# Final norm: rows read ahead of the last two experts' sums, both experts' rows gathered and scattered apart

## The chip, the core and the metric

The kernel runs on one core of one Trainium2 chip, as one launch. The metric is device time in microseconds (us). The engines are TensorE (PE), VectorE (DVE), ScalarE (ACT), GpSimd (POOL) and SyncE (SP); SP does no arithmetic and issues most of the plain transfers, in its program's order. Indirect transfers (gather, scatter, scatter with add) are issued by POOL. Sixteen DMA engines move the data.

## The reference

One decoder block on 1024 tokens of width 1024, float32: attention, then a mixture of experts, then a last norm. What matters here is its end (cut):

```python
def _rmsnorm(x, g):
    y = x * lax.rsqrt(jnp.mean(x * x, axis=-1, keepdims=True) + NORM_EPS)
    return y * g
...
    h2 = _modulate(_rmsnorm(x, g_ffn[layer]), shift_ffn, scale_ffn).reshape(b * s, d)
    y = _hierarchical_moe(h2, ...)          # top group of 4, top 2 of its 8 experts
    x = x + gate_ffn[:, None, :] * y
    return _rmsnorm(x, g_final)
```

Each token gets the weighted outputs of two of the 32 experts (SwiGLU, inner width 512), added to its row; the row is then divided by its root mean square and multiplied by `g_final`.

## The kernel before

The program first computes attention and the routing, and leaves the rows of x, without the experts' part, in a DRAM tensor `acc` (1024 x 1024). The expert stage then runs over 32 places e = 0 to 31 (a table made on the chip says which expert stands at which place; every second place from 5 on has lists of up to 64 rows, the others up to 96; below, the expert at place e is called expert e). For each place POOL gathers the rows (`load_x`, L1220), PE turns them round (`xpose`), multiplies with 8 blocks of gate and up weights (`gate_up`) and 4 blocks of down weights (`down`); DVE multiplies by the gate row into `ys` (`finish`, L1322 and L1328), and POOL adds `ys` to the rows of `acc` by an indirect transfer (`add_rows`, L1337). A list `order` sets how the steps of neighbouring places mix. Weight blocks of 512 KB are loaded by SP (`load_to`, L974), up to 34 blocks ahead of their use; each of the last twelve waits for the load three before it.

Buffers of 128 x 1024 floats come from one pool of 49, taken in turn (`slot`). A framework adds the waits: for a buffer's last users, and between any two transfers that touch the same DRAM tensor when one of them writes it.

The tail, around the change: `finish(30)` issues the add of place 30 and then calls `f_load`, which lets SP read all of `acc` into eight buffers `fx0` to `fx7` (L1351), and lets POOL gather the rows of place 31 from `acc` into `xlast` (L1353). The sums of place 31 itself are never added in `acc`: `xl_add` (L1406) adds them to `xlast` on DVE. Then `f_square` (L1359, ACT) squares a tile and sums each row into a column of `ssf`; `rsqrt` (L172 to L187) makes the reciprocal roots of some columns, in 12 steps on DVE or 15 on POOL; `f_out` (L1364) multiplies on DVE, and SP writes 128 rows of the output (L1365). The rows of `xlast` are done the same way (column 8) and scattered over the output by POOL (L1369), behind all eight plain outputs, which wrote those rows without the sums of place 31.

The string `TAIL` sets the order of this part: sN is a square, rA-B roots of columns A to B-1 on DVE, gA-B the same on POOL, oN an output, y is `finish(31)`, x is `xl_add`. The squares of fx0 to fx2 stand ahead of it, between the down products of place 31. A last test (L1431 to L1438) asks whether any list ran over; the branch is not taken here.

Of the kernel before, what the change touches and what calls it, by code (L numbers as in the profile page):

```python
# [7 lines left out]
F32 = mybir.dt.float32  # L8
# [5 lines left out]
ALU = mybir.AluOpType  # L14
# [4 lines left out]
T = 1024  # L19
D = 1024  # L20
KT = 8
NE = 32
CAP = 96
CAPS = 64
# [33 lines left out]
UF = [1, 1, 1, 1, 1, 1, 0.98, 0.91]  # L58
GE = 'GGGG'
QS = "AS"  # L60
TAIL = "s3 s4 s5 r0-3 o0 y o1 g3-6 o2 s6 s7 x o3 o4 g6-9 o5 o6 o7 o8"
XA, TA, DA = 6, 4, 5
LLX = 34
LT = 0
# [32 lines left out]
def build(nc, tc, I, out, cap=CAP):  # L97
# [6 lines left out]
    cp = pool("const", 1)  # L104
# [5 lines left out]
    V, A, G, PE = nc.vector, nc.scalar, nc.gpsimd, nc.tensor  # L110
# [19 lines left out]
    def slot(name, dt=F32):  # L130
        return up.tile([128, D], dt, name=name, tag="u")
# [92 lines left out]
    for o in LOADS0.split():  # L224
        if o[0] == "w":
            i = int(o[1])
# [93 lines left out]
    acc = dp.tile([T, D], F32, name="acc")  # L320
# [285 lines left out]
    bc = {}  # L606
# [339 lines left out]
    EW, XE, ST, EREG = {}, {}, {}, {}  # L946
    capof = lambda e: CAPS if e in SMALL else cap
    listof = lambda e: (ls if e < NF else lsP)[:capof(e), e:e + 1]
# [119 lines left out]
    for k in range(KT):  # L1068
# [39 lines left out]
        for i in (0, 1):  # L1108
            hi, lo = wsp[i]
            for half in (0, 1):  # L1110
                c = slice(half * 512, half * 512 + 512)
# [11 lines left out]
    i = 0  # L1123
# [31 lines left out]
    for which in (0, 1):  # L1155
        qk_alloc(0, which)
        for half in (0, 1):
            c = slice(half * 512, half * 512 + 512)
# [7 lines left out]
    pend, last, fresh, late = list(range(NS)), [], set(), []  # L1166
    for s_ in range(NS + L7 + 1):
        if s_ < NS:
            p, i = divmod(s_, 16)
# [42 lines left out]
        last = todo  # L1212
# [101 lines left out]
    def finish(e):  # L1314
        st, c = ST.pop(e), capof(e)
        ps = st["y"]
        ys = slot(f"ys{e}")
        g = bc["gate2"]
        halves = [(slice(h * 512, h * 512 + 512), h) for h in (0, 1)]
        for n, h in halves:  # L1320
            r = slice(h * 64, h * 64 + 64)
            V.tensor_mul(ys[0:64, n], ps[r, 0:512], g[r, n])  # L1322
        if c > 64:
            t = slot(f"yt{e}")[0:64, 0:512]
            others(t, ps)
            for n, h in halves:
                r = slice(h * 32, h * 32 + 32)
                V.tensor_mul(ys[64:96, n], t[r], g[r, n])  # L1328
        if e == NE - 1:
            ST["last"] = ys  # L1330
        else:
            add_rows(e, ys)
        if e == NE - 2:
            f_load()

    def add_rows(e, ys):
        G.indirect_dma_start(out=acc[:], out_offset=bass.IndirectOffsetOnAxis(ap=listof(e), axis=0),  # L1337
# [1 line left out]
                             compute_op=ALU.add)  # L1339


    ssf = cp.tile([128, KT + 1], F32, name="ssf")
    rf = cp.tile([128, KT + 1], F32, name="rf")
    G.memset(ssf, 1.0)
    FX, FY = [], {}

    def f_load():
        load_to(len(wseq))
        for tt in range(KT):
            x = slot(f"fx{tt}")  # L1350
            nc.sync.dma_start(x, acc[tt * 128:tt * 128 + 128, :])  # L1351
            FX.append(x)
        G.indirect_dma_start(out=XL[:CAPS], out_offset=None, in_=acc[:],  # L1353
                             in_offset=bass.IndirectOffsetOnAxis(ap=listof(NE - 1), axis=0),
                             bounds_check=T - 1, oob_is_err=False)

    def f_square(tt, x, n=128):
        FY[tt] = slot(f"fy{tt}")
        A.activation(FY[tt][:n], x[:n], AF.Square, accum_out=ssf[:n, tt:tt + 1])  # L1359

    def f_out(tt):
        y = FY.pop(tt)
        if tt < KT:
            V.scalar_tensor_tensor(y, FX[tt], rf[:, tt:tt + 1], bc["final"], op0=ALU.mult, op1=ALU.mult)  # L1364
            nc.sync.dma_start(out[tt * 128:tt * 128 + 128, :], y)  # L1365
        else:
            V.scalar_tensor_tensor(y[:CAPS], XL[:CAPS], rf[:CAPS, tt:tt + 1], bc["final"][:CAPS],
                                   op0=ALU.mult, op1=ALU.mult)
            G.indirect_dma_start(out=out[:], out_offset=bass.IndirectOffsetOnAxis(ap=listof(NE - 1), axis=0),  # L1369
                                 in_=y[:CAPS], in_offset=None, bounds_check=T - 1, oob_is_err=False)  # L1370

    LL = LLX
    load_x(0)
# [6 lines left out]
    for o in order:  # L1380
        kind, e, i = o
        if kind in "GD":
            load_to(max(loaded[0], wpos[o] + LL - wpos[o] * LT // len(wseq)))
        if kind == "G":
            gate_up(e, i)
        elif kind == "X":
            xpose(e)
            if e + 1 < NE:
                scale_x(e + 1)
            if e + 2 < NE:  # L1390
                load_x(e + 2)
        elif kind == "T":
            act_t(e)
        elif kind == "D":
            down(e, i)
        elif kind == "Y" and e < NE - 1:
            finish(e)
        if o == ("G", NE - 2, 4):
            spread_row("final", cols[:, 72:80], G)
            XL = slot("xlast")  # L1400
            G.memset(XL[:CAPS], 0.0)
        if e == NE - 1 and kind == "D" and i:
            f_square(i - 1, FX[i - 1])

    def xl_add():
        V.tensor_add(XL[:CAPS], XL[:CAPS], ST["last"][:CAPS])  # L1406
        f_square(KT, XL, CAPS)

    sq_ = lambda tt: f_square(tt, FX[tt])
    rs_ = lambda a, b, eng=V: rsqrt(rf[:, a:b], ssf[:, a:b], b - a, 1.0 / D, eng)  # L1410
    for st in TAIL.split():
        k, a = st[0], [int(x) for x in st[1:].split("-") if x]
# [25 lines left out]
    with tc.If(rv > 0):  # L1438
# [15 lines left out]
        with tc.For_i(0, NE, 1) as e:  # L1454
# [6 lines left out]
            for tt in range(KT):  # L1461
                c = slice(tt * 128, tt * 128 + 128)
                x, xt, act, y, a = work2[tt % 2]
# [34 lines left out]
        for tt in range(KT):  # L1498
            x = fx[tt]
# [81 lines left out]
```

## Time and profile before

| | us |
|---|---|
| median of 3 runs | 1341.71 (1338.05 to 1342.66) |
| profiled execution | 1341.36 |
| its span | 1339.5 |
| busy in it: PE, DVE, ACT, POOL | 1170.3, 746.9, 520.3, 237.4 |
| data moved by DMA | 304.5 MB, mean 227 GB/s |

The span runs from the first to the last instruction; the execution's time is a little longer than it. A view of the profile names an instruction by engine, line and what it writes and reads (`fx<-acc`). "Landing" of a transfer is the time from its issue until its semaphore says that all is there. The chain that ended last is followed back from the last instruction, at each link to what released it, so it shows the work that sets the end; busy time of engines off that chain is not lost time.

### The profile page before, as it was taken

Reading aid. Unit: us, or ns where it says so; the run is one execution under the profiler, and the core shown is the slowest. Engines: PE = TensorE matmul, PEld = TensorE weight load, DVE = VectorE, ACT = ScalarE, POOL = GpSimd, SP = SyncE. Lnnn points to the kernel's source line nnn. Section 1 sums busy time; section 2 is a strip of 40 time slices with the busy share of each in tenths; the row PEclk is TensorE's granted clock in tenths of the full one; section 3 lists DMA queues with packets and bytes.
Section 4 is the critical chain, followed back from the end, with each engine's and each line's share of the span. In section 5 each row is a group of like instructions: output and inputs, shape, how many; then the busy total and the mean of one; then the engine's idle time right before and its main releaser. Section 6 shows DMA issues by size and latency. Waiting matters only on the chain. (4 is left out here: it accounts for less than half of the span.)

```text
span 1339.5 us, 19457 instructions
## 1 busy us (share of the span) xinstructions
PE 1170.3 (87%) x6848; PEld 688.1 (51%) x6848; DVE 746.9 (56%) x1484; ACT 520.3 (39%) x1023; POOL 237.4 (18%) x296
## 2 busy tenths in 40 slices
PE   4699989999999999799887999899999998888970
PEld 3497778778866886577665422223233222222320
DVE  6958773865497858878867233333333333332324
ACT  5246553655655445435422322233222222222212
POOL 3600000120100002313231110111111111111203
PEclk9799999999999999899998899999999999999985
DMA  9422442441001010456666799999999999999985
GB/s 353 161 77 95 149 154 95 142 85 42 32 17 48 16 64 0 149 214 236 229 250 228 253 334 359 336 386 377 367 372 373 376 375 374 376 377 388 359 276 200
DMA packets 89384, 304.54 MB, mean 227 GB/s; under 512 B 12417, under 2 KB 14849, under 8 KB 89282
## 3 DMA queue, kind: packets, MB, share of 16 engines
q1 hardware_dynamic: 81778, 282.00, 57.2%
q0 software_dynamic: 6352, 17.05, 5.4%
q10 hardware_dynamic: 1152, 4.19, 0.8%
q8 instruction: 56, 0.92, 0.3%
q14 instruction: 46, 0.38, 0.1%
HBM read 278.30 MB, written 29.63 MB: 230 GB/s over the span
## 5 line engine op out<-in xcount | busy, mean ns | idle before, releaser
L1264 PE MATMUL gu<-ew,xs 128*64 128x512 f32 x1024 | 252.1, 612 | 9.2 <-DMA ew<-we 5.2
L1322 DVE TENSOR_TENSOR ys<-y,bc_gate 64x512 f32<-64x512 f32 x64 | 44.0, 688 | 218.0 <-PE y L1271 129.0
L1264 PE MATMUL y<-ew,at 128*64 128x512 f32 x512 | 127.9, 629 | 12.1 <-DMA ew<-we 10.7
L1264 PEld LDWEIGHTS gu<-ew,xs 128*64 128x64 f32 x1024 | 63.6, 138 | 145.0 <-issue 73.1
L1241 ACT ACTIVATE xs<-xp,modc,affn 128x96 f32<-128x96 f32 (+1 forms) x128 | 52.0, 420 | 157.5 <-PE xp L1253 89.7
L549 PE MATMUL tp<-ident,P 128*128 128x128 f32 x576 | 89.1, 280 | 20.1 <-DVE P L533 9.6
L1337 POOL DMA_INDIRECT acc<-ys,lsP x27 | 38.7, 1434 | 377.7 <-DVE ys L1328 236.0
L532 DVE TENSOR_TENSOR_SCAN K<-K 128x1024 f32<-128x1024 f32 (+7 forms) x64 | 95.4, 1491 | 5.9 <-ACT K L520 5.7
L1264 PEld LDWEIGHTS y<-ew,at 128*64 128x64 f32 x512 | 35.8, 142 | 97.1 <-issue 45.3
L549 PEld LDWEIGHTS tp<-ident,P 128*128 128x128 f32 x576 | 65.7, 141 | 38.6 <-issue 9.4
L516 ACT ACTIVATE P<-P,st 128x1024 f32<-128x1024 f32 (+7 forms) x64 | 50.0, 781 | 91.3 <-DVE st L514 45.6
L573 PE MATMUL o<-PT,v 128*64 128x256 f32 (+1 forms) x640 | 74.9, 374 | 10.1 <-DVE PT L554 7.1
L1239 DVE TENSOR_SCALAR xs<-xp,affn,modc 128x96 f32<-128x96 f32 (+1 forms) x128 | 45.5, 363 | 57.8 <-ACT xs L1241 57.2
L210 DVE CUSTOM_DVE_ANT_0 wada<-wada,sc 128x1024 f32<-128x1024 f32 x48 | 64.4, 1354 | 9.7 <-DMA wada<-w_adaT 9.4
L520 ACT ACTIVATE K<-S 128x1024 f32<-128x1024 f32 (+7 forms) x64 | 41.9, 655 | 71.5 <-PE S L503 34.4
L1271 PE MATMUL gu<-ew,xs 128*32 128x512 f32 x576 | 69.3, 598 | 0.0
L514 DVE CUSTOM_DVE_ANT_0 P<-S,B 128x1024 f32<-128x1024 f32 (+7 forms) x64 | 48.3, 756 | 36.9 <-PE S L501 32.8
L1276 ACT ACTIVATE yt<-y 64x512 f32<-64x512 f32 x18 | 10.7, 595 | 143.4 <-PE xp L1253 127.1
L573 PEld LDWEIGHTS o<-PT,v 128*64 128x64 f32 x640 | 45.4, 141 | 40.1 <-DVE PT L554 9.7
L552 ACT ACTIVATE PT<-tp 128x512 f32<-128x512 f32 (+3 forms) x120 | 56.2, 496 | 15.4 <-PE tp L549 14.5
L533 DVE TENSOR_TENSOR P<-P,K 128x1023 f32<-128x1023 f32 (+7 forms) x64 | 51.6, 806 | 5.7 <-ACT P L521 0.7
L554 DVE COPY PT<-tp 128x512 f32<-128x512 f32 (+3 forms) x72 | 37.3, 537 | 16.1 <-PE tp L549 15.8
(637 smaller groups left out, 2510.0 us busy)
## 6 DMA issues: line engine op xcount, KB each, us to landing
ew<-we SPq DMA_DIRECT2D x384, 512.0 KB, 10.5
wada<-w_adaT SPq DMA_DIRECT2D x48, 512.0 KB, 6.0
wqk<-wqk SPq DMA_DIRECT2D x16, 512.0 KB, 3.6
xT<-xT SPq DMA_DIRECT2D x16, 256.0 KB, 5.5
wv<-wv SPq DMA_DIRECT2D x8, 512.0 KB, 7.7
B<-bias SPq DMA_DIRECT2D x8, 512.0 KB, 5.3
wo<-w_out SPq DMA_DIRECT2D x8, 512.0 KB, 4.9
x<-x SPq DMA_DIRECT2D x8, 512.0 KB, 4.7
```

The lines of the kernel that those rows point to most:

```text
L210: V.tensor_tensor_reduce(w, w, sc, op0=ALU.mult, op1=ALU.add, scale=1.0, scalar=0.0, accum_out=modc[:, v * 8 + k:v * 8 + k + 1])
L514: V.tensor_tensor_reduce(e, s, Bt[p, hd][:, :L], op0=ALU.add, op1=ALU.min, scale=-0.125, scalar=BIG, accum_out=st[:, 0:1])
L516: A.activation(e, e, AF.Exp, bias=st[:, 0:1], scale=-1.0, accum_out=st[:, 2:3])
L532: V.tensor_tensor_scan(k[:, :L], k[:, :L], k[:, :L], 1.0, op0=ALU.mult, op1=ALU.bypass)
L533: V.tensor_mul(b[:, 1:L], b[:, 1:L], k[:, 0:L - 1])
L549: PE.transpose(tp[:, jl - 4 * x, :], e[:, (jl - qo) * 128:(jl - qo) * 128 + 128], ident)
L552: A.activation(dst, tp[:, j0 - 4 * x:j1 - 4 * x, :], AF.Copy)
L573: PE.matmul(ps[hd * 64:hd * 64 + 64, 0:w], VV[p][:, j, hd * 64:hd * 64 + 64], pt[hd][jl // 4][:, jl % 4, 0:w], start=(n == 0), stop=(n == ...
L1239: V.tensor_scalar(dst, src, affn[:, k:k + 1], modc[:, 24 + k:25 + k], op0=ALU.mult, op1=ALU.add)
L1241: A.activation(dst, src, AF.Identity, scale=affn[:, k:k + 1], bias=modc[:, 24 + k:25 + k])
L1264: PE.matmul(ps[h * 64:h * 64 + 64, 0:512], a[:, i, 0:64], w[:, h * 512:h * 512 + 512], start=(i == 0), stop=(i == n - 1))
L1271: PE.matmul(ps[r:r + 32, 512:1024], a[:, j, 64:96], w[:, h * 512:h * 512 + 512], start=(j < 2), stop=(j >= n - 2))
```

## The change

`f_load` is called by `finish(29)`, ahead of the add of place 30, and no longer holds the gather. After the add of place 30, `finish(30)` issues two gathers from `acc`, the rows of place 30 and those of place 31 (`xlast30`, 96 rows, and `xlast31`, 64 rows). `fx0` to `fx7` hold the rows without the sums of places 30 and 31. Place 30's rows get column 8 of `ssf`, place 31's column 9, and both are scattered over the output, 30 first. `TAIL` changes: the square of `xlast31` comes ahead of s6, s7 and s8 (s8 is the square of `xlast30`), and the roots of columns 6 to 9 go from POOL to DVE.

```diff
--- before.py
+++ after.py
@@ -58,7 +58,7 @@
 UF = [1, 1, 1, 1, 1, 1, 0.98, 0.91]
 GE = 'GGGG'
 QS = "AS"
-TAIL = "s3 s4 s5 r0-3 o0 y o1 g3-6 o2 s6 s7 x o3 o4 g6-9 o5 o6 o7 o8"
+TAIL = "r0-3 o0 o1 s3 s4 s5 g3-6 o2 y x s6 s7 s8 o3 o4 o5 r6-10 o6 o7 o8 o9"
 XA, TA, DA = 6, 4, 5
 LLX = 34
 LT = 0
@@ -1330,8 +1330,13 @@
             ST["last"] = ys
         else:
             add_rows(e, ys)
-        if e == NE - 2:
+        if e == NE - 3:
             f_load()
+        elif e == NE - 2:
+            for i in (NE - 2, NE - 1):
+                G.indirect_dma_start(out=XL[i][:capof(i)], out_offset=None, in_=acc[:],
+                                     in_offset=bass.IndirectOffsetOnAxis(ap=listof(i), axis=0),
+                                     bounds_check=T - 1, oob_is_err=False)
 
     def add_rows(e, ys):
         G.indirect_dma_start(out=acc[:], out_offset=bass.IndirectOffsetOnAxis(ap=listof(e), axis=0),
@@ -1339,10 +1344,10 @@
                              compute_op=ALU.add)
 
 
-    ssf = cp.tile([128, KT + 1], F32, name="ssf")
-    rf = cp.tile([128, KT + 1], F32, name="rf")
+    ssf = cp.tile([128, KT + 2], F32, name="ssf")
+    rf = cp.tile([128, KT + 2], F32, name="rf")
     G.memset(ssf, 1.0)
-    FX, FY = [], {}
+    FX, FY, XL = [], {}, {}
 
     def f_load():
         load_to(len(wseq))
@@ -1350,9 +1355,6 @@
             x = slot(f"fx{tt}")
             nc.sync.dma_start(x, acc[tt * 128:tt * 128 + 128, :])
             FX.append(x)
-        G.indirect_dma_start(out=XL[:CAPS], out_offset=None, in_=acc[:],
-                             in_offset=bass.IndirectOffsetOnAxis(ap=listof(NE - 1), axis=0),
-                             bounds_check=T - 1, oob_is_err=False)
 
     def f_square(tt, x, n=128):
         FY[tt] = slot(f"fy{tt}")
@@ -1364,10 +1366,11 @@
             V.scalar_tensor_tensor(y, FX[tt], rf[:, tt:tt + 1], bc["final"], op0=ALU.mult, op1=ALU.mult)
             nc.sync.dma_start(out[tt * 128:tt * 128 + 128, :], y)
         else:
-            V.scalar_tensor_tensor(y[:CAPS], XL[:CAPS], rf[:CAPS, tt:tt + 1], bc["final"][:CAPS],
-                                   op0=ALU.mult, op1=ALU.mult)
-            G.indirect_dma_start(out=out[:], out_offset=bass.IndirectOffsetOnAxis(ap=listof(NE - 1), axis=0),
-                                 in_=y[:CAPS], in_offset=None, bounds_check=T - 1, oob_is_err=False)
+            e = NE - 2 + tt - KT
+            c = capof(e)
+            V.scalar_tensor_tensor(y[:c], XL[e][:c], rf[:c, tt:tt + 1], bc["final"][:c], op0=ALU.mult, op1=ALU.mult)
+            G.indirect_dma_start(out=out[:], out_offset=bass.IndirectOffsetOnAxis(ap=listof(e), axis=0),
+                                 in_=y[:c], in_offset=None, bounds_check=T - 1, oob_is_err=False)
 
     LL = LLX
     load_x(0)
@@ -1397,16 +1400,18 @@
             finish(e)
         if o == ("G", NE - 2, 4):
             spread_row("final", cols[:, 72:80], G)
-            XL = slot("xlast")
-            G.memset(XL[:CAPS], 0.0)
+            for i in (NE - 2, NE - 1):
+                XL[i] = slot(f"xlast{i}")
+                G.memset(XL[i][:capof(i)], 0.0)
         if e == NE - 1 and kind == "D" and i:
             f_square(i - 1, FX[i - 1])
 
     def xl_add():
-        V.tensor_add(XL[:CAPS], XL[:CAPS], ST["last"][:CAPS])
-        f_square(KT, XL, CAPS)
-
-    sq_ = lambda tt: f_square(tt, FX[tt])
+        x = XL[NE - 1][:CAPS]
+        V.tensor_add(x, x, ST["last"][:CAPS])
+        f_square(KT + 1, x, CAPS)
+
+    sq_ = lambda tt: f_square(tt, FX[tt]) if tt < KT else f_square(tt, XL[NE - 2], cap)
     rs_ = lambda a, b, eng=V: rsqrt(rf[:, a:b], ssf[:, a:b], b - a, 1.0 / D, eng)
     for st in TAIL.split():
         k, a = st[0], [int(x) for x in st[1:].split("-") if x]
```

What the built programs hold at three places follows. A row is line, operation, written from read, size, and the semaphores that it waits for: DMAHW0 to 7 are those of SP's transfers, taken in turn (fx0 to fx7 use 0 to 7, and so do the eight plain outputs), DMASW those of POOL's.

SP's queue, behind the weight loads, before: the last weight block and the reads of `acc`.

```order
L974 DMA ew31_11_10496<-we 128x1024 [waits DMAHW4_49,PE_49]
L1351 DMA fx0_10701<-acc_305 128x1024 [waits DMASW6_49,PE_49,Activation_49]
L1351 DMA fx1_10703<-acc_305 128x1024 [waits PE_49]
L1351 DMA fx2_10705<-acc_305 128x1024 [waits PE_49]
L1351 DMA fx3_10707<-acc_305 128x1024 [waits DVE_49]
L1351 DMA fx4_10709<-acc_305 128x1024 [waits DVE_49]
```

The same place in the changed program:

```order
L974 DMA ew31_11_10496<-we 128x1024 [waits DMAHW4_49,PE_49]
L1356 DMA fx0_10620<-acc_305 128x1024 [waits DMASW5_49,PE_49]
L1356 DMA fx1_10622<-acc_305 128x1024 [waits PE_49]
L1356 DMA fx2_10624<-acc_305 128x1024 [waits PE_49,Activation_49]
L1356 DMA fx3_10626<-acc_305 128x1024
L1356 DMA fx4_10628<-acc_305 128x1024 [waits PE_49]
```

The reads stand at the same place in SP's queue; the first waits for another add (DMASW5, place 29, instead of DMASW6, place 30).

POOL's queue from the clearing of `xlast` to the first roots, before:

```order
L1401 MEMSET xlast_10601 64x1024 [waits DMAHW3_49,DMAHW5_49,DMAHW2_49,PE_49]
L1337 DMA acc_305<-ys29_10612,lsP_316 1024x1024 [waits DMASW5_49,DMASW4_49,DVE_49]
L1337 DMA acc_305<-ys30_10690,lsP_316 1024x1024 [waits DMASW5_49,DVE_49]
L1353 DMA xlast_10601<-acc_305,lsP_316 64x1024 [waits DMASW7_49,DMASW6_49,Pool_49]
L172 TENSOR_SCALAR rs_10783<-ssf_7010 128x3 [waits Activation_49]
```

POOL's queue there in the changed program:

```order
L1405 MEMSET xlast30_10601 96x1024 [waits DMAHW3_49,DMAHW5_49,DMAHW2_49,PE_49]
L1405 MEMSET xlast31_10603 64x1024 [waits DMAHW4_49,PE_49]
L1342 DMA acc_305<-ys29_10614,lsP_316 1024x1024 [waits DMASW5_49,DMASW4_49,DVE_49]
L1342 DMA acc_305<-ys30_10708,lsP_316 1024x1024 [waits DMAHW3_49,DMAHW4_49,DMAHW2_49,DMAHW5_49,DMAHW1_49,DMAHW6_49,DMAHW0_49,DMAHW7_49,DMASW5_49,DVE_49]
L1337 DMA xlast30_10601<-acc_305,lsP_316 96x1024 [waits DMASW7_49,DMASW6_49,Pool_49]
L1337 DMA xlast31_10603<-acc_305,lsP_316 64x1024 [waits Pool_49]
L172 TENSOR_SCALAR rs_10785<-ssf_7010 128x3 [waits Activation_49]
```

The add of place 30 (`ys30`) now waits for all eight of SP's semaphores, at the values of the eight reads, and a second gather has come in behind it.

POOL's queue at the end of the changed program, from the last steps of its one set of roots on (before, a second set and one scatter stood there):

```order
L186 TENSOR_SCALAR rs_10785<-rs_10785 128x3 [waits Pool_49]
L187 TENSOR_TENSOR rf_7011<-rs_10785 128x3 [waits Pool_49]
L1372 DMA out<-fy8_10813,lsP_316 1024x1024 [waits DMAHW3_49,DMAHW4_49,DMAHW2_49,DMAHW5_49,DMAHW1_49,DMAHW6_49,DMAHW0_49,DMAHW7_49,DMASW1_49,DVE_49]
L1372 DMA out<-fy9_10807,lsP_316 1024x1024 [waits DMASW1_49,DVE_49]
L1442 TENSOR_LOAD cmi_10851 [waits DVE_49]
```

The first scatter waits for the eight plain outputs, as the one scatter did before; the second waits for the first (DMASW1).

ACT's squares, before:

```order
L1359 ACTIVATE fy3_10757,ssf_7010<-fx3_10707 128x1024 [waits DMAHW3_49]
L1359 ACTIVATE fy4_10759,ssf_7010<-fx4_10709 128x1024 [waits DMAHW4_49,Activation_49]
L1359 ACTIVATE fy5_10761,ssf_7010<-fx5_10711 128x1024 [waits DMAHW5_49,DMASW4_49,DMASW0_49]
L1359 ACTIVATE fy6_10801,ssf_7010<-fx6_10713 128x1024 [waits DMAHW6_49]
L1359 ACTIVATE fy7_10803,ssf_7010<-fx7_10715 128x1024 [waits DMAHW7_49]
L1359 ACTIVATE fy8_10806,ssf_7010<-xlast_10601 64x1024 [waits DMASW5_49,DMASW4_49,DVE_49]
```

ACT's squares in the changed program:

```order
L1361 ACTIVATE fy4_10781,ssf_7010<-fx4_10628 128x1024 [waits DMAHW4_49,DMASW4_49,DMASW0_49]
L1361 ACTIVATE fy5_10783,ssf_7010<-fx5_10630 128x1024 [waits DMAHW5_49]
L1361 ACTIVATE fy9_10807,ssf_7010<-xlast31_10603 64x1024 [waits DMAHW7_49,DVE_49]
L1361 ACTIVATE fy6_10809,ssf_7010<-fx6_10632 128x1024 [waits DMAHW6_49,DMASW5_49]
L1361 ACTIVATE fy7_10811,ssf_7010<-fx7_10634 128x1024 [waits DMAHW7_49]
L1361 ACTIVATE fy8_10813,ssf_7010<-xlast30_10601 96x1024 [waits DMASW7_49]
```

The square of the last place's rows, which waits for DVE's add, has moved ahead of those of fx6, fx7 and the second gathered tile.

## Rows read from the trace of the kernel before

**Rows 1.** The page: the span, and GB/s in 40 slices of it.
```profile
span 1339.5 us, 19457 instructions
...
GB/s 353 161 77 95 149 154 95 142 85 42 32 17 48 16 64 0 149 214 236 229 250 228 253 334 359 336 386 377 367 372 373 376 375 374 376 377 388 359 276 200
```

**Rows 2.** The chain that ended last: start us, length us, what.
```profile
1291.75 6.45 DMA acc<-ys,lsP
...
1300.08 8.75 DMA fx<-acc
...
1324.98 0.21 POOL rf L187
...
1327.72 2.63 DMA out<-fy
```

**Rows 3.** SP's own waits, 1230 to 1340: us in total, times, longest.
```profile
SPq L1351 <- DMA acc<-ys,lsP: 7.3, 1, 7.3
```

**Rows 4.** Timeline of ACT, 1255 to 1262: start us, length us, instruction.
```profile
1259.63 0.59 ACT L1289 ACTIVATE sg<-gu 64x512 f32<-64x512 f32 x1
```

**Rows 5.** Timeline of POOL, 1250 to 1340: the add of place 29.
```profile
1270.41 1.47 POOL L1337 DMA_INDIRECT acc<-ys,lsP x1 [6.34 <-DVE ys L1322]
```

**Rows 6.** Line 974 in 1290 to 1292, the last weight load: ns, start us; landing.
```profile
L974 SPq DMA_DIRECT2D ew<-we x1: 333/333/333, 1290.6 to 1290.6; - x1
...
DMA to landing us min/median/max: 4.1/4.1/4.1
```

**Rows 7.** Line 1351, the eight reads: ns min/median/max, first and last start; landing.
```profile
L1351 SPq DMA_DIRECT2D fx<-acc x8: 331/430/462, 1298.3 to 1301.6; - x8
...
DMA to landing us min/median/max: 4.2/8.8/10.9
```

**Rows 8.** A stretch: us, PE, PEld, DVE, ACT, POOL busy, clock, DMA share, GB/s.
```profile
1255.00:1260.00 5.00, 4.82 (x26) 1.25 (x26) 2.89 (x7) 2.60 (x5) 3.23 (x5) 1.00 1.02 417
```

**Rows 9.** Line 1353, the gather of place 31.
```profile
L1353 POOL DMA_INDIRECT xlast<-acc,lsP x1: 1012/1012/1012, 1299.0 to 1299.0; - x1
...
DMA to landing us min/median/max: 7.4/7.4/7.4
```

**Rows 10.** Line 1337, all 31 adds.
```profile
DMA to landing us min/median/max: 5.6/7.9/9.2
```

**Rows 11.** Line 1369, the scatter of place 31.
```profile
L1369 POOL DMA_INDIRECT out<-fy,lsP x1: 1011/1011/1011, 1331.2 to 1331.2; - x1
...
DMA to landing us min/median/max: 3.6/3.6/3.6
```

**Rows 12.** Line 1220, the 32 gathers of the expert stage.
```profile
DMA to landing us min/median/max: 4.6/8.1/10.5
```

**Rows 13.** Timeline of DVE, 1306 to 1330: roots, last sums, last two plain outputs.
```profile
1307.65 0.17 DVE L172 TENSOR_SCALAR rs<-ssf 128x3 f32<-128x3 f32 x1 [14.10 <-ACT fy L1359]
...
1309.64 0.16 DVE L184 SCALAR_TENSOR_TENSOR rf<-rs 128x3 f32<-128x3 f32 x1
...
1315.07 1.21 DVE L1406 TENSOR_TENSOR xlast<-xlast,ys 64x1024 f32<-64x1024 f32 x1
...
1325.22 2.48 DVE L1364 SCALAR_TENSOR_TENSOR fy<-fx,rf,bc_final 128x1024 f32<-128x1024 f32 x2 [3.44 <-POOL rf L187]
```

**Rows 14.** Timeline of ACT, 1300 to 1320: two squares in a row.
```profile
1310.14 1.06 ACT L1359 ACTIVATE fy<-fx 128x1024 f32<-128x1024 f32 x1
...
1311.29 1.06 ACT L1359 ACTIVATE fy<-fx 128x1024 f32<-128x1024 f32 x1
```

**Rows 15.** Timeline of POOL, 1310 to 1319: first, seventh and last step of one set of roots.
```profile
1311.39 0.19 POOL L172 TENSOR_SCALAR rs<-ssf 128x3 f32<-128x3 f32 x1 [11.40 <-ACT fy L1359]
...
1313.01 0.99 POOL L187 TENSOR_TENSOR rs<-rs 128x3 f32<-128x3 f32 x1
...
1317.87 0.19 POOL L187 TENSOR_TENSOR rf<-rs 128x3 f32<-128x3 f32 x1
```

**Rows 16.** Line 1575, the program's end: POOL's drains, ns min/median/max.
```profile
L1575 POOLq DRAIN  x3: 46/107/5381, 1333.3 to 1339.2; - x3
```

## The prediction

> **What bounds the kernel now.** I read the page first, then the chain that ended last, then the waits and the timeline of its stretch. The profiled execution took 1341.36 us around a span of 1339.5 us; the median of the three runs, 1341.71, is 0.35 us above it, so sums made on the profile may stand against the median as they are. Up to about 1295 us the expert stage streams weights at some 370 GB/s [rows 1], and nothing there is touched: the rows of PE stand in the same order in both programs, and every weight load stands where it stood. What the change reaches is the serial tail behind it. The reader is to see these links in it [rows 2]: the add of expert 30's rows takes 6.45 us from its start at 1291.75 to its landing at 1298.20; the eight reads of `acc` follow, with a link of 8.75 us; the reciprocal roots on POOL end at 1325.2; the last plain output leaves at 1327.72 and lands at 1330.35; then comes the scatter of the last expert's rows. The reads began late for one reason: SP waited 7.3 us for that add [rows 3]. This is the wait that the change takes away.
>
> **Part 1: the reads go earlier, by 7.4 us.** In the new program the first read waits for the add of expert 29, which starts at 1270.4 [rows 5], and for buffers whose last users are done at 1259.6, when expert 29's activation starts [rows 4]. But SP works in order, and ahead of the reads stand the weight loads, the last of which was issued at 1290.6 and took 0.33 us [rows 6]. So the reads start at 1290.9 where they started at 1298.3 [rows 7]. Before, the last of them was issued at 1301.6 and landed 10.9 us later, at 1312.5 [rows 7]; moved as a block by 7.4 us this is **1305.1**. Short end: the last weights land 4.1 us after 1290.6, at 1294.7 [rows 6], and eight reads then follow at the 1.23 us in which 512 KB pass near 420 GB/s, the rate of an unthrottled weight stretch [rows 8]: 1304.5. Long end: the weight loads still on their way (three of 0.5 MB, of which I take 1 MB as not yet moved) use 2.5 us of the queue first: 1307.6. I take the middle value, since the reads before had a gather of 0.26 MB beside them which is now gone.
>
> **Part 2: a new wait takes the place of the old one.** The reads now stand ahead of the add of expert 30 in the program, and the add writes the tensor that they read. In the built program that add waits for the eight semaphores DMAHW0 to 7, which are those of the eight reads. It could start at 1291.75; now it starts behind the last landing. Queued behind it on POOL are the two gathers, and behind these the roots for rows 3 to 5. Behind the gather of expert 31 hang DVE's add of the last sums (and o3 to o5 in DVE's queue), and on ACT the square of those rows, behind which s6, s7 and s8 are queued. So two indirect transfers, which ran under PE and under the reads before, come in series after the reads.
> Costs: POOL starts 0.8 us after a landing (1298.20 to 1299.0 at the old gather [rows 2, 9]), so the add starts at 1305.9. It lands after 6.45 as at 1291.75 [rows 2]; over all adds this was 5.6 to 9.2, median 7.9 [rows 10], mostly under full weight traffic, while here only o0 to o2 are written meanwhile: 1312.35. The first gather starts at 1313.15 and holds POOL for 1.0 us [rows 9], the second starts at 1314.15. Its landing is bounded by 3.6 us (the scatter of as many rows with no other traffic [rows 11]) and 7.4 us (the same gather under the reads [rows 9]); the fastest of the earlier gathers took 4.6 under weights [rows 12]. The queues are idle by then, but the gather of 96 rows stands in front, so I take 4.1: **1318.25**.
>
> **Part 3: from the gather to the last plain output.** DVE's add, 0.1 + 1.2 us [rows 13]: 1319.55. Four squares on ACT in a row (x, 6, 7, 8), 1.15 us from start to start [rows 14]: 1324.2. The roots for four columns go to DVE instead of POOL: 1307.65 to 1309.80 for three columns [rows 13], so 0.1 + 2.15: 1326.45. That saves POOL's 6.7 us for 15 steps [rows 15], of which the path had the last stretch. o6 and o7 need 0.1 + 2.5 (two in 2.48 [rows 13]): 1329.05. The last output issues and lands in 0.06 + 2.63 [rows 2]: **1331.75**, against 1330.35. The outputs o8 and o9 (2.5 us) lie under this transfer. POOL's roots for 3 to 5 start near 1315.2 and take 4.1 us when no step is stretched, 6.7 when some are, as the one of 0.99 us was [rows 15]; o3 to o5 (3.7 us) then end at 1323.2 to 1325.7, under the squares, or 1.1 us past the point where DVE should take up its roots. I take nothing for it and keep 1.1 for the range.
>
> **Part 4: a second scatter, in series.** The scatter of expert 30's rows waits for all eight outputs; that of expert 31 waits for the landing of the first, since a token may be in both lists. First scatter: 0.85 us after the last landing, as before (1330.35 to 1331.2 [rows 2, 11]): 1332.6; landing 3.6 later [rows 11]: 1336.2; 0.8 us to POOL's next start: the last scatter starts at **1337.0** instead of 1331.2. This part alone is 4.4 us, with no cover: nothing else is left to run. After the last scatter's start the span went on for 8.3 us, most of it in a drain of 5.4 us on POOL [rows 16]; I leave that as it is. Two more columns in the small tiles and a second clearing of a buffer (POOL idles before the add of expert 29) cost nothing on the path.
> **Sum:** 1337.0 - 1331.2 = 5.8 us; 1341.36 + 5.8 = **1347.2 us**, 0.4% slower. Its terms: reads 7.4 us earlier; add, gathers and their starts behind the reads; the last plain output 1.4 us later for all that; the second scatter 4.4.
>
> **A page against these rows.** The final scatter moved 64 rows (0.26 MB) in 3.6 us [rows 11]. The Trainium skill (DMA: Bandwidth & Descriptors, Anatomy of one DMA — SWDGE (gpsimd) path) fits an indirect-capable transfer with 2.0 us and its bytes at 436 GB/s: an estimate from it is 2.6 us for this one, 2.9 for the add and 3.5 for both gathers. Its sum would be 1341.1, no change at all; the one row with idle queues is 1.0 us above the page, so that end gets the small chance that the first rival gives it.
>
> **The rivals.**
> *Idle queues make the indirect steps cheap.* The add and the gathers now run after the reads, not under weights. If the add lands like the scatter, in 3.6 + 0.3 us for 96 rows instead of 64 [rows 11], and the gather in 3.6, the path loses 2.55 + 0.5: 1344.2. POOL's roots may then become what is late, which gives up to 1 us back. For it: no weight traffic is left. Against it: no add of the trace went below 5.6 [rows 10], an add reads and writes, and o0 to o2 (1.5 MB) are written at the same time. Its far end, 1341 to 1342, needs every indirect step near 3 us; the smallest of them took 3.6 with the queues to itself [rows 11], so that end holds 0.03 of this case's 0.21.
> *The reads gain nothing or the indirect steps stay dear.* If the first read waits for anything that is as late as before, the block does not move: 1347.2 + 7.4 = 1354.6. If it moves, but lands at 1307.6, the add takes its median and the gather its 7.4: 2.5 + 1.45 + 3.3 more, 1354.4. For it: the medians. Against it: buffers and the earlier add are early [rows 4, 5], and the queues empty towards 1309.
> *The other side: the wait for the reads costs nothing.* If the add were issued at 1291.75 as before, under the reads, it would land in about 8 us and the gather in 7.4 more [rows 9, 10], near 1309.1; then x, squares, roots, o7 and both scatters end the span at 1336.0, a time of 1337.9. The point at which slower turns into faster is a last read landing at 1299.3. With reads that start at 1290.9 that is 4.2 MB in 8.4 us behind 1 MB of weights, 620 GB/s, where the best stretch shows 417 [rows 8]; so this needs the wait not to bind at all.
>
> **How the numbers follow.** Forecast 0.68, cheap indirect steps 0.21, dear ones 0.07, wait without cost 0.04. A measurement of this kernel tells about 0.3% (4 us) from no change, so "slower" begins at 1345.7 and "faster" ends at 1337.7. The forecast's low terms together (reads 0.6, add 0.85, gather 0.5, start of the last scatter 0.5) give 1344.7; the runs before spread over 4.6 us, so 1 us more goes under it: low 1343.5. Its high terms (reads 2.5, add 1.45, gather 3.3, roots 1.1) will not all fall together; half of them gives 1351.4. Slower: 0.07, nine tenths of 0.68 and 0.04 of the first rival: 0.72. Faster: most of the last case, 0.03. Same: 0.25.
>
> **What would show it.** In the profile after: reads from about 1290.9; the add of expert 30 starting within 1 us of the last read's landing, near 1306; the wait for the gather ending DVE's idle time before the add of the last sums near 1318; two scatters 4 to 5 us apart at the end; POOL without a second set of roots. The forecast is wrong if the reads start at 1298, if the add runs beside the reads, if the indirect steps land in 3 us, or if the drain at the end shrinks or grows with two scatters.

## The result, and the profile after

The changed kernel took 1346.79 us (median of 6 runs, 1345.18 to 1350.89), the kernel before 1339.46 beside it (median of 6, 1336.29 to 1342.66). The ratio is 1.006, with a 95% interval of 1.0041 to 1.0079: 7.3 us slower. The forecast was 1347.2 us, slower.

One caution on levels. The forecast stood on an execution of before at 1341.36 us, above its median, so the change it forecast was 5.8 us, and 7.3 were measured. The profiled execution of after, 1350.89 us, is the longest of its six. Its expert stage ran 1.2 us later than that of before: the last gate and up products start at 1288.31, and before they started at 1287.11. Executions of one kernel differ by that much and more (those of before by 6.4 us above). So times inside the tail are compared below from the start of the first read of `acc`, and across kernels the medians are compared.

In the changed kernel the adds are at L1342, the gathers of `xlast` at L1337, the reads at L1356, the squares at L1361, the plain outputs at L1366 and the scatters at L1372.

The chain that ended last (start us, length us, what) went through SP's reads, behind the add, in [rows 2]. Here it stays on POOL from the add to the roots, by way of the issue of both gathers; then come DVE's outputs, and both scatters, one behind the other, at its end:

```profile
1308.45 1.62 DMA acc<-ys,lsP
1310.07 5.32 issue
...
1315.61 1.04 POOL xlast L1337
...
1316.95 0.97 POOL xlast L1337
...
1322.90 0.21 POOL rf L187
...
1324.33 2.48 DVE fy L1366 x2
...
1328.95 2.49 DVE fy L1366 x2
1331.46 2.65 DMA out<-fy
...
1334.99 4.80 DMA out<-fy,lsP
...
1340.90 0.63 POOL out L1372
```

"Issue" for 5.32 us is time in which the profile shows nothing that POOL waits for. It is the rest of the add's way to its landing: 1.62 + 5.32 = 6.9 us, of which 6.4 go to the landing; POOL starts on the next gather 0.8 us after it.

POOL's waits from 1280 to 1349 (us in total, times, longest) say which wait took the place of SP's 7.3 us of [rows 3]:

```profile
POOL acc L1342 <- DMA fx<-acc: 35.1, 1, 35.1
POOL out L1372 <- DVE cmi L1440: 11.9, 1, 11.9
POOL xlast L1337 <- issue: 5.8, 2, 5.5
POOL out L1372 <- DMA out<-fy,lsP: 4.6, 1, 4.6
```

The add of place 30 now waits for the reads. Most of those 35.1 us cost nothing, since its rows `ys30` are complete only at 1292.7 (1291.32 + 1.38, below). What lies between that and 1308.45, 15.7 us, is the delay that the new wait brings; how much of it costs time, e1 shows below. The last line is the second scatter behind the first. The 11.9 us are put down to DVE, but the plain outputs that the scatter also waits for land at 1334.1, 0.9 us ahead of its start.

The timeline around the add and the gathers (start us, length us, instruction, in brackets the idle time before it and what ended it), of SP, DVE and POOL:

```profile
1292.00 5.74 SPq L1356 DMA_DIRECT2D fx<-acc  x8
...
1291.32 1.38 DVE L1328 TENSOR_TENSOR ys<-yt,bc_gate 32x512 f32<-32x512 f32 x2
...
1308.79 1.39 DVE L1322 TENSOR_TENSOR ys<-y,bc_gate 64x512 f32<-64x512 f32 x2
1321.22 1.22 DVE L1411 TENSOR_TENSOR xlast<-xlast,ys 64x1024 f32<-64x1024 f32 x1 [11.05 <-issue]
...
1308.45 1.62 POOL L1342 DMA_INDIRECT acc<-ys,lsP  x1 [35.13 <-DMA fx<-acc]
1315.61 1.04 POOL L1337 DMA_INDIRECT xlast<-acc,lsP  x1 [5.54 <-issue]
1316.95 0.97 POOL L1337 DMA_INDIRECT xlast<-acc,lsP  x1 [0.30 <-issue]
```

The landing of the add (L1342), then that of the two gathers (L1337):

```profile
DMA to landing us min/median/max: 6.4/6.4/6.4
...
DMA to landing us min/median/max: 4.2/4.2/4.2
```

Before, the last sums were added at 1315.07, with no idle time ahead of them [rows 13]. Now DVE stands idle for 11 us ahead of the same add. The profile names nothing that ended this wait ("issue"), but the second gather landed at 1321.15 (1316.95 + 4.2), just ahead of it. How empty this stretch is shows in the busy time by stretches (us, then PE, PEld, DVE, ACT and POOL busy, clock, DMA share, GB/s):

```profile
1308.20:1315.60 7.40, 0.00 (x0) 0.00 (x0) 1.93 (x3) 0.00 (x0) 1.62 (x1) 0.50 0.75 205
1315.60:1321.20 5.60, 0.00 (x0) 0.00 (x0) 0.00 (x0) 0.00 (x0) 4.40 (x14) 0.50 0.41 112
```

For 13 us PE and ACT do nothing, DVE 1.9 us of work, and POOL issues three transfers and takes roots. The same add and the old gather used to run under PE's last products and under the reads.

From the first read's start to the span's end, before took 41.2 us (1298.28 to 1339.5) and after 57.1 (1292.00 to 1349.1): 15.9 us more tail, behind reads that start 6.3 us earlier.

### The profile page after: what moved, and what is told of

Same layout as the page of the kernel before. It is cut to its first block, busy times and chain, and to the rows that moved or that the text cites. A ratio compares the mean times of both kernels' runs of the same rounds, so it can differ in the third digit from the quotient of the medians.

```text
span 1349.1 us, 19470 instructions
## 1 busy us (share of the span) xinstructions
PE 1170.0 (87%) x6848; PEld 687.2 (51%) x6848; DVE 749.3 (56%) x1497; ACT 519.8 (39%) x1025; POOL 233.0 (17%) x284
## 5 line engine op out<-in xcount | busy, mean ns | idle before, releaser
L1322 DVE TENSOR_TENSOR ys<-y,bc_gate 64x512 f32<-64x512 f32 x64 | 44.0, 688 | 222.2 <-PE y L1271 123.0
L1342 POOL DMA_INDIRECT acc<-ys,lsP x27 | 39.0, 1444 | 393.9 <-DVE ys L1328 215.5
L1239 DVE TENSOR_SCALAR xs<-xp,affn,modc 128x96 f32<-128x96 f32 (+1 forms) x128 | 45.5, 363 | 56.2 <-ACT xs L1241 49.5
```

Source lines behind the costliest of these rows:

```text
L1239: V.tensor_scalar(dst, src, affn[:, k:k + 1], modc[:, 24 + k:25 + k], op0=ALU.mult, op1=ALU.add)
```

## The experiments

Three theories went in. **W**: the add's wait for the reads puts add and gathers in series behind them, and the second scatter adds its own length. **S**: only the second scatter costs, and the wait is covered by work that was late anyway. **O**: the order of the tail is what costs (plain outputs 3 to 7 and roots on POOL behind the gather). "Tail" below is the time from the first read's start to the span's end.

| kernel | what differs | median us (before beside it) | tail us |
|---|---|---|---|
| before | | 1339.46 to 1340.43, beside the others | 41.2 |
| after | | 1346.79 (1339.46) | 57.1 |
| e1_reads_x1d | after, reads don't hold the add | 1338.84 (1339.63) | 48.8 |
| e2_one_scatter | after, one scatter | 1342.41 (1339.63) | 52.1 |
| e5_both | after, both of these | 1335.41 (1340.43) | 45.2 |
| e8_half | after, half the reads hold the add | 1343.01 (1340.43) | 51.7 |
| e3_reads_after_add | after, reads back behind the add | 1345.12 (1339.63) | 46.3 |
| e4_tail | after, another order of the tail | 1340.54 (1339.63) | 49.5 |
| e6_before_two_scatters | before, its scatter issued twice | 1344.13 (1340.43) | 44.9 |
| e9_roots_on_dve | before, POOL's roots on DVE | 1338.70 (1339.52) | 39.0 |
| e7_before_tail | before, another order of the tail | 1332.32 (1340.43) | 36.9 |
| e10_before_tail_again | the same program again | 1334.51 (1339.52) | 36.0 |

### Without the wait: e1_reads_x1d

```diff
-            nc.sync.dma_start(x, acc[tt * 128:tt * 128 + 128, :])
+            nc.sync.dma_start(x, x1d[tt * 128:tt * 128 + 128, :])
```

The same bytes are read at the same place in SP's queue, from a tensor that no add writes. (Taking only the wait away would be a race.)

> The changed kernel, but the eight early reads take the rows of x1d (x ahead of the experts) instead of acc; the output so lacks the experts' sums in rows that are not scattered. The reads have the same size and place, but the add of expert 30 no longer waits for them. Theory W (the add's wait for the reads, then gathers and a second scatter in series): the add starts near 1292, the gathers land near 1309 to 1310 instead of 1321, DVE's add of the last sums comes 11 us earlier, and all behind it; 1335 to 1337 us. Rival S (only the second scatter costs; the wait for the reads is covered, since ACT and DVE are busy with those reads): no change against the changed kernel, about 1347.

Measured: 1338.84 us, ratio to before 1.000 (0.9988 to 1.0012), 8.0 us less than after; the tail is 8.4 us shorter. POOL's and DVE's timeline:

```profile
1292.50 1.44 POOL L1342 DMA_INDIRECT acc<-ys,lsP  x1 [19.89 <-DVE ys L1328]
1302.57 1.04 POOL L1337 DMA_INDIRECT xlast<-acc,lsP  x1 [8.63 <-issue]
1303.91 0.97 POOL L1337 DMA_INDIRECT xlast<-acc,lsP  x1 [0.30 <-issue]
...
1312.23 1.22 DVE L1411 TENSOR_TENSOR xlast<-xlast,ys 64x1024 f32<-64x1024 f32 x1 [0.81 <-DVE ys L1322]
...
DMA to landing us min/median/max: 8.1/8.1/8.1
```

The add starts as soon as its rows are there, which is what ends its wait now. Counted from the first read (1291.35 here), the last sums are added 8.3 us earlier (20.9 us against 29.2), which is what came off the tail. S, by which this kernel stays near 1347, falls. W missed its upper bound by 2 us: the gathers landed 8.1 us after their issue (the last line above), as gathers do under transfers [rows 12], where after's landed in 4.2 on idle queues. The wait costs 8 us, not the 15.3 by which the add starts later after the first read (16.45 against 1.15): the late add landed in 6.4 us instead of 9.3 and the late gathers in 4.2 instead of 8.1, because the queues had become free, and that gives 6.8 us back.

The other tensor could also have made the reads themselves faster. The gain does not come from there: the sixth square, of fx5, starts 15.2 us after the first read in e1 (first line) and 13.2 in after (second line).

```profile
1306.50 1.06 ACT L1361 ACTIVATE fy<-fx 128x1024 f32<-128x1024 f32 x1
...
1305.24 1.06 ACT L1361 ACTIVATE fy<-fx 128x1024 f32<-128x1024 f32 x1
```

### Without the second scatter: e2_one_scatter, and both: e5_both

```diff
             V.scalar_tensor_tensor(y[:c], XL[e][:c], rf[:c, tt:tt + 1], bc["final"][:c], op0=ALU.mult, op1=ALU.mult)
+            if e == NE - 2:
+                return
             G.indirect_dma_start(out=out[:], out_offset=bass.IndirectOffsetOnAxis(ap=listof(e), axis=0),
```

> The changed kernel without the scatter of expert 30's rows (their square, root and product stay; the output lacks expert 30's sums). Theory W: the last scatter follows the plain outputs at once, which takes away the first scatter's landing and the step to the next, 4.4 to 5.6 us: 1341 to 1342.5 us, still above the kernel before (1339.5). Rival S: the whole loss goes, 1339 to 1340.

Measured: 1342.41 us, ratio 1.0022 (1.0006 to 1.0038): 4.4 us less than after, and a tail 5.0 us shorter. By S nothing would have been left of the 7.3 us; 2.8 were.

e5_both is both edits in one kernel.

> The changed kernel with both costs taken away: reads from x1d (the add waits for nothing), and no scatter of expert 30's rows (so the output lacks the experts' sums in rows not scattered, and expert 30's in its rows). Theory W with costs that add: 1346.8 - 8.0 (reads from x1d) - 4.4 (one scatter) = 1334.4 us, 1333 to 1336; that is what the earlier reads would bring alone, some 5 us against the kernel before. Rival: the two share one cost, so that taking both away gives hardly more than one, 1338 to 1339.

Measured: 1335.41 us, ratio 0.9962 (0.9947 to 0.9977), a tail 11.9 us shorter than after's. Within a microsecond the two costs add: 8.0 + 4.4 = 12.4 by the medians, 11.4 together. It also prices what the early reads are worth where nothing is paid for them: 5.0 us less than before.

### The wait in another dose: e8_half

```diff
-            nc.sync.dma_start(x, acc[tt * 128:tt * 128 + 128, :])
+            nc.sync.dma_start(x, (acc if tt < KT // 2 else x1d)[tt * 128:tt * 128 + 128, :])
```

> The changed kernel with the first four reads from acc and the last four from x1d (rows of the last four tiles lack the experts' sums unless scattered). The add of expert 30 waits for four reads instead of eight. Theory W (the wait is the cost, and its length counts): the add starts 4.5 to 5 us earlier, under the other four reads, and lands after 7 to 8 us instead of 6.4; 3 to 4.5 us less than the changed kernel, 1342.3 to 1343.8. Rival (only whether there is a wait counts, or what follows is bound elsewhere): 1346 to 1347, or 1339 as without a wait.

Measured: 1343.01 us, ratio 1.002 (1.0002 to 1.0037). The add on POOL's timeline, behind a first read at 1287.35:

```profile
1299.10 1.44 POOL L1342 DMA_INDIRECT acc<-ys,lsP  x1 [29.93 <-DVE rs L182]
```

The profile puts this wait down to DVE, but the add waits for four reads, and the last of them, fx3, is squared from 1298.41 on. The add starts 11.75 us after the first read, where it was 16.45 in after (1292.00 to 1308.45), and lands in 6.0 us, not in the 7 to 8 expected under the other four reads. With 4.7 us less of waiting the tail is 5.4 us shorter, the median 3.8. The cost grows with the wait. This alone would not exclude an effect of the second tensor, which has half its share of the reads here too; the squares of e1 speak against that.

### The reads back behind the add: e3_reads_after_add

```diff
-        if e == NE - 3:
+        if e == NE - 2:
             f_load()
-        elif e == NE - 2:
             for i in (NE - 2, NE - 1):
```

> The changed kernel with the eight reads put back behind the add of expert 30 (as before); two gathers, two scatters and the new order of the tail stay. Theory W: add near 1292, reads from 1298.3, gathers under the reads, x added near 1316; last plain output lands near 1328, then two scatters: 1344 to 1345.5 us, some 2 us less than the changed kernel, so that the earlier reads are worth less than nothing here. If the earlier reads gained anything: above 1347. Rival S: as the changed kernel, 1346 to 1348.

Measured: 1345.12 us, ratio 1.0043 (1.0025 to 1.0062), 5.5 us more than before. So the change without its early reads costs 5.5 us, and with them 7.3. The intervals of the two overlap: the early reads, with the wait that they bring, gained nothing, and that they made the kernel slower still is not shown. POOL's end:

```profile
1330.21 1.04 POOL L1371 DMA_INDIRECT out<-fy,lsP  x1 [11.84 <-DVE cmi L1439]
1335.21 0.93 POOL L1371 DMA_INDIRECT out<-fy,lsP  x1 [3.96 <-DMA out<-fy,lsP]
```

The first scatter starts 32.8 us after the first read (1297.39), as in before (32.9, 1298.3 to 1331.2 [rows 7, 11]); the second follows 5.0 us later, and the kernel is 5.5 us longer. That is all that differs at the end.

### The second scatter alone, in the kernel before: e6_before_two_scatters

```diff
-            G.indirect_dma_start(out=out[:], out_offset=bass.IndirectOffsetOnAxis(ap=listof(NE - 1), axis=0),
-                                 in_=y[:CAPS], in_offset=None, bounds_check=T - 1, oob_is_err=False)
+            for _ in (0, 1):
+                G.indirect_dma_start(out=out[:], out_offset=bass.IndirectOffsetOnAxis(ap=listof(NE - 1), axis=0),
+                                     in_=y[:CAPS], in_offset=None, bounds_check=T - 1, oob_is_err=False)
```

> The kernel before with its last scatter issued twice, the same 64 rows (nothing is left out). It prices a second scatter in series by itself. Theory W: 3.6 to 4.8 us to land and 0.8 us to the next start, 1339.6 + 4.0 to 5.6 = 1343.6 to 1345.2 us. Rival (the drain on POOL at the end covers part of it, or grows with each scatter): below 1342.5 or above 1346.5.

Measured: 1344.13 us, ratio 1.0027 (1.0012 to 1.0043), 3.7 us more than before, a tail 3.7 us longer. POOL's timeline:

```profile
1330.95 1.00 POOL L1370 DMA_INDIRECT out<-fy,lsP  x1 [6.03 <-SPq L1439]
1334.53 0.91 POOL L1370 DMA_INDIRECT out<-fy,lsP  x1 [2.58 <-DMA out<-fy,lsP]
```

The two stand 3.6 us apart, and the program is that much longer. A scatter at the end has no cover. The price lies under the 4.0 to 5.6 us expected; the time itself fell into its range because the kernel before took 0.8 us more beside this run than assumed. The distance was 3.6 us behind 64 rows, and 5.0 to 5.6 behind the 96 rows of place 30 in e3 and after. Not all of that is rows: the two scatters here landed in 3.2 and 3.3 us, so POOL's next start came some 0.3 us after the landing, and in after 0.8.

### The order of the tail: e4_tail, e9, e7 and e10

In the changed kernel, with all its transfers kept:

```diff
-TAIL = "r0-3 o0 o1 s3 s4 s5 g3-6 o2 y x s6 s7 s8 o3 o4 o5 r6-10 o6 o7 o8 o9"
+TAIL = "r0-3 o0 o1 s3 s4 s5 o2 r3-6 s6 s7 y o3 o4 o5 r6-8 o6 o7 s8 r8-9 o8 x r9-10 o9"
```

> The changed kernel, nothing left out, with another order of the tail: o2, the roots of columns 3 to 5 (on DVE), o3 to o5, s6, s7, the roots of 6 and 7, o6 and o7 all ahead of the add of the last sums, and expert 30's rows ahead of expert 31's. Theory O (the wait for the reads costs only because plain outputs 3 to 7 are queued behind the gather on DVE and ACT): the plain outputs are done near 1323, the first scatter starts at 1324 to 1325 instead of 1335, the second near 1330: 1335.5 to 1337.5 us, below both kernels. If instead the chain of add, gathers and scatters itself sets the end (W without O): 1341 or more.

Measured: 1340.54 us, ratio 1.0011 (0.9995 to 1.0027), 6.3 us less than after: the wait and the second scatter are still there, but the plain outputs (and their roots, moved from POOL to DVE) no longer stand behind the gathers. So another order gets back most of the loss. O missed its range by 3 us, and the result lies half a microsecond from the bound of the other case. How much of the 6.3 us is the wait and how much the order by itself is not separated: the kernel before gains 5 us from another order too (e10, below), and there no add waits for reads. The chain of e4_tail (start us, length us, what):

```profile
1304.04 1.55 DMA acc<-ys,lsP
...
1311.09 6.62 DMA xlast<-acc,lsP
...
1321.02 1.28 DVE fy L1371
1322.30 1.14 DVE xlast L1411
1323.47 1.16 ACT fy L1361 x2
...
1326.76 1.28 DVE fy L1371
...
1328.32 0.94 POOL out L1372
```

With the plain outputs out of the way the chain runs from the add through the first gather and the work on the two sets of gathered rows to the last scatter, which is close to the other case of the expectation. The first gather landed 6.6 us after its issue instead of 4.2, with plain outputs written beside it, and the last sums, their square, a set of roots and an output stand one behind the other at the end.

In the kernel before, first the roots alone, from POOL to DVE at the same places (`g` to `r` in `TAIL`; "that run" is e7, which follows below):

> The kernel before with POOL's two sets of roots made by DVE at the same places of the order; last sums and squares stay where they were. Nothing is left out. If POOL's roots were the whole of what the other order of the tail brought: as that run, 1331 to 1335 us. If it was the order (last sums ahead of the first roots, one set of roots fewer) with DVE's work as the bound: DVE takes on 4.3 us of steps and loses 5.3 us of waits, 1338 to 1340 us.

Measured: 1338.70 us, ratio 1.000 (0.9985 to 1.0016). So POOL's slower roots, a link of before's chain [rows 2], were worth nothing clear of noise: 0.8 us by the medians, 2.2 us in the tail of one trace, an interval of 2 us to either side. With the last sums put first and one set of roots, on DVE, for columns 3 to 8:

```diff
-TAIL = "s3 s4 s5 r0-3 o0 y o1 g3-6 o2 s6 s7 x o3 o4 g6-9 o5 o6 o7 o8"
+TAIL = "y x r0-3 s3 s4 s5 s6 s7 o0 o1 o2 r3-9 o3 o4 o5 o6 o7 o8"
```

> The kernel before, nothing left out and reads where they were, with another order of its tail: last sums added before the first roots, all squares in a row, the roots of columns 3 to 8 in one set on DVE, none on POOL. Theory O (in the kernel before the plain outputs wait for POOL's two sets of roots, 5.3 us of DVE's idle time): DVE works through, the last plain output starts near 1322.6 and the span ends 4 to 5 us earlier, 1334.5 to 1336.5 us. Rival (the tail is bound by DVE's work or by the reads, the roots are covered): 1338.5 to 1340.5.

Measured: 1332.32 us, ratio 0.9934 (0.9915 to 0.9954), better than expected, while its tail of 36.9 us was 4.3 us shorter than before's. Since these two did not agree, the same program was run again:

> The same program as the one with the other order of the tail, run again beside the kernel before: that run gave 8 us where the working of its tail gives 4 to 5, on few runs. If the larger figure is a property of the program: 0.5 to 0.7% less again. If it was the spread of the runs: 0.3 to 0.4% less, 4 to 5.5 us.

Measured: 1334.51 us, ratio 0.997 (0.9957 to 0.9983), 5.0 us less than before, with a tail of 36.0 us, 5.2 us shorter. Two sets of runs give 5 and 8 us by the medians (4 and 9 by the ratios), two traces 4 and 5; I take 5. It computes the whole of the reference and beats both kernels. Its timeline of DVE and POOL:

```profile
1301.22 1.22 DVE L1406 TENSOR_TENSOR xlast<-xlast,ys 64x1024 f32<-64x1024 f32 x1 [6.91 <-DMA xlast<-acc,lsP]
...
1311.12 6.07 DVE L1364 SCALAR_TENSOR_TENSOR fy<-fx,rf,bc_final 128x1024 f32<-128x1024 f32 x5
...
1320.86 0.95 POOL L1369 DMA_INDIRECT out<-fy,lsP  x1 [25.92 <-SPq L1438]
```

The five outputs o3 to o7 run without a break (before, 3.4 us of idle time stood ahead of the last two [rows 13]), and the scatter starts 27.6 us after the first read (1293.24), where it was 32.9 in before (1298.3 to 1331.2 [rows 7, 11]).

## Why the prediction was right, step by step

**The mechanism held.** The runs show its two prices apart: the wait 8.0 us (e1) and the second scatter 4.4 (e2; 3.7 for 64 rows in e6, where 4.4 was forecast). Against them stand early reads that would be worth 5.0 us (e5). 8.0 + 4.4 - 5.0 = 7.4, and 7.3 were measured. That the two agree to 0.1 us is luck: e5 itself puts the two costs at 11.4, and the kernel before took 1.0 us more beside e5 than beside after. The rival by which the wait costs nothing would need e1 to be no faster than after; it put a kernel that loses nothing by the wait at 1337.9, and e1, with the wait taken away, took 1338.84.

That 1347.2 and 1346.79 lie so close is luck too. The sum stood on an execution 1.9 us above the median of before, and its change of 5.8 us was 1.5 too small.

**The terms in after's own trace**, forecast beside measured:

| step | forecast | after |
|---|---|---|
| first read starts | 1290.9 | 1292.00 |
| first read to the add's start | 15.0 | 16.45 |
| add, issue to landing | 6.45 | 6.4 |
| landing to the next POOL start | 0.8 | about 0.75 |
| second gather, issue to landing | 4.1 | 4.2 |
| four squares, to the roots on DVE | 4.6 | 4.3 |
| POOL's roots 3 to 5, o3 to o5 | end under the squares | end with them, at 1326.8 |
| last plain output lands | 1331.75 | 1334.1 |
| first scatter, issue to landing | 3.6 | 4.80 |
| last scatter starts | 1337.0 | 1340.60 |
| from there to the span's end | 8.3 | 8.5 |

The last scatter came 3.6 us later than forecast. 1.1 of it is the first read, for this execution's expert stage ran 1.2 us late. Of the rest, two terms were too small. The sign of two scatters 4 to 5 us apart missed for the same reason: they stand 5.6 us apart.

**The reads, 1.4 us too small.** I moved them as a block, 3.3 us from the first issue to the last [rows 7]. Here they are stretched over 5.4 us, and the last landed some 10.3 us after its issue where I had 10.9. Line 1356, the reads (ns, first and last start), then SP's waits ahead of them (us in total, times, longest):

```profile
L1356 SPq DMA_DIRECT2D fx<-acc x8: 319/438/632, 1292.0 to 1297.4; - x8
```

```profile
SPq L1356 <- DMA ew<-we: 1.5, 1, 1.5
...
SPq L1356 <- ACT sg L1289: 0.5, 1, 0.5
SPq L1356 <- PE gu L1264: 0.5, 1, 0.5
```

I had looked at what the first read waits for [rows 4, 5]; the later ones wait too, for weights that are still landing and for the engines that use them. Counted from the first read, the far end of my range for the last landing (1307.6, from 1 MB of weights ahead, so 16.7 us) covered it: the add's last semaphore wait was over near 1307.7, after 15.7 us.

**The first scatter, 1.2 us too small.** I gave the scatter of place 30 the landing of the one of place 31, though it moves 96 rows and not 64. Line 1372 (landing, us min/median/max of the two):

```profile
DMA to landing us min/median/max: 3.2/4.0/4.8
```

The second scatter, of 64 rows, landed in 3.2, the first in 4.8. What this is made of stays open: e5's only scatter, of 64 rows, took 4.6, so the number of rows is not the whole of it.

The Trainium skill (DMA: Bandwidth & Descriptors, Anatomy of one DMA — SWDGE (gpsimd) path) gives 2.0 us and the bytes at 436 GB/s, an estimate of 2.6 us for 64 rows and 2.9 for 96; no scatter here was under 3.2, and the one of 96 rows in after took 4.8. By that page's figures the kernel would not have become slower, and the measurement decides against them.

**The edge that held by luck.** "Covered" for POOL's roots was true with nothing to spare. Their last steps (start us, length us) run beside DVE's add of the last sums:

```profile
1318.00 0.19 POOL L172 TENSOR_SCALAR rs<-ssf 128x3 f32<-128x3 f32 x1
...
1321.32 1.18 POOL L182 TENSOR_TENSOR rs<-rs 128x3 f32<-128x3 f32 x1
...
1322.90 0.21 POOL rf L187
...
1323.13 3.68 DVE L1366 SCALAR_TENSOR_TENSOR fy<-fx,rf,bc_final 128x1024 f32<-128x1024 f32 x3 [0.69 <-POOL rf L187]
...
1326.77 0.17 DVE L172 TENSOR_SCALAR rs<-ssf 128x4 f32<-128x4 f32 x1
```

o3 to o5 end at 1326.81, the squares at 1326.74, and DVE takes up its roots at 1326.77. The chain of after goes through POOL and not through the squares for this reason: the two were level. The 1.1 us that the prediction kept for this should have been 1.4 (1325.7 against 1324.3). Two more of its figures are off by little: 512 KB at 417 GB/s pass in 1.26 us, not 1.23, and the low end, 1344.7 less 1, is 1343.7. None of the three moves the forecast.

**What stays open.** A version with early reads and no wait was run only with work left out (e1, e5). The rows of place 30 could be carried to those of place 31 on the chip, without going through `acc`; the second scatter would stay, so by e1's time that alone gains nothing. It was not tried. The second gather was not run by itself either: in after it puts the gather of place 31 and POOL's roots 1.3 us later (1315.61 to 1316.95), which is part of the price of the wait here.

## What to carry to other kernels

Moving a read of a DRAM tensor ahead of a write to it did not take a wait away here, it turned it round: the writer, and all that is queued behind it on its engine, then waits for the last of the reads to land, so price what hangs behind the write before moving the read. A transfer at the program's end, with nothing left to run beside it, cost its whole time to landing, 3.2 to 4.8 us for 64 or 96 rows. Where a tail is a chain of short steps, its order can be worth as much as a transfer: 5 us came from putting the latest input's work first and the roots into fewer sets, on DVE, with nothing removed, and 4.4 from leaving a scatter out.

## What the runs showed of the hardware

- **An indirect gather's landing follows what else is on the queues.** The same gathers landed in 4.2 to 4.8 us on idle queues (after, e2, e8), 6.6 beside the plain outputs (e4), 8.1 beside reads (e1), 8.7 in e3 and 9.5 to 9.9 in e5. So making an indirect transfer earlier gave back part of what it gained: counted from the first read, e1 issued its gathers 12.4 us earlier and had its sums 8.3 us earlier.
- **Steps of the roots on POOL stretch beside some operations of DVE.** The step of 0.20 us took 1.18 at 1321.32, beside DVE's add of two tiles at 1321.22 to 1322.44, the pattern of the 0.99 us in [rows 15], which ran beside DVE's outputs. Beside DVE's product at L1322 in before (1311.22 to 1312.61), one of whose inputs is TensorE's result, the steps kept their 0.19 to 0.24 us.
- **The roots of one column on DVE were no cheaper.** Twelve steps took 2.15 us for three columns [rows 13] and 2.15 for four (1326.77 to 1328.92 in after); six took 2.2 in e10 (1308.91 to 1311.08). In e4 a set for one column, which is built from other instructions, took 2.1 (1318.91 to 1320.98). So one set for many columns is the cheapest form.
